# Twenty series of extra products in one group of layer 0's up projection

## The chip, the cores and the metric

The kernel runs on one core of one Trainium2 chip. The metric is the time of one execution in device microseconds (us). A core has a matrix engine, TensorE (PE in the profile), which multiplies a stationary operand of up to 128 columns (the weights, loaded ahead of each product; PEld in the profile) with the moving rows that stream past it and adds into PSUM; VectorE (DVE), ScalarE (ACT) and GpSimd (POOL) for elementwise work; and SyncE (SP), which here issues the loads of weights from HBM into SBUF, the on-chip memory. The engines run side by side and wait for each other by semaphores.

## The reference

A small decoder of two layers on 256 tokens, with 16 learned tokens put ahead of them, so that T = 272 rows; the width is 2048, with 16 heads of 128 and an MLP of 8192.

```python
for layer in range(DEPTH):
    a = rms_norm(h, norm_attn[layer])
    if layer < N_A_LAYERS:                      # layer 0
        proj = a @ fox_w_in[i]                  # q, k, v and forget gates
        o = forgetting_attention(...)
        h = h + o.reshape(b, length, D_MODEL) @ fox_w_o[i]
    else:                                       # layer 1
        c = rms_norm(h, kv_norm)
        k_s, v_s = jnp.split(c @ w_kv, 2, axis=-1)
        q = split_heads(a @ sb_w_q[i])
        o = stick_breaking_attention(q, shared_k, shared_v)
        h = h + o.reshape(b, length, D_MODEL) @ sb_w_o[i]
    h = h + squared_relu_mlp(rms_norm(h, norm_mlp[layer]), w_up[layer], w_down[layer])
return rms_norm(h, final_norm)[:, N_META:]
```

`squared_relu_mlp` is `jnp.square(jax.nn.relu(h @ w_up)) @ w_down`. Everything is float32.

## The kernel before

Activations are kept transposed, features on the 128 partitions and tokens along the row, in 16 chunks of 128 features. Every large matrix product goes through `gemm_group` (L173): one call makes 512 output features (four accumulators `acc`, one per 128 features, `m`) from all 2048 input features, in four steps `kb` of four chunks each. A float32 product is made of three products of a narrower type, float32r: both operands are split into a high part and the remainder, and high times high, high times low and low times high are added. So each pair of an input chunk `kc` and an accumulator `m` takes three products.

The activations lie split in a tile `x_...` made by `Split` (L99): per chunk 640 numbers of 4 bytes, in which the high part stands at `sp.hi` and the low part at `sp.lo`. 64 numbers are 256 bytes, and a chunk is ten such pieces. In layer 0, where the rows are 272 long (`t0` = 0), the high part begins at number 48 of a chunk and the low part at 368, so that both end at the end of a piece and touch five. In layer 1, where only the 256 rows of the tokens are needed (`t0` = 16), they begin at 0 and 320, at the beginning of a piece, and touch four.

The weights of a step `kb` come from HBM in two halves `raw` (512 KB each) on SP's queue (L197). ScalarE rounds a half into `whi` (L214) and VectorE writes the remainder into `wlo` (L215); each has two chunks of 512 columns. There are four buffers of `raw`, of `whi` and of `wlo`, that is two steps' worth. In layer 0 the weights begin at the beginning of a piece, so that the 128 columns of a product touch two pieces; in layer 1 they begin 16 numbers later and touch three.

The products are issued at L235 to L238 through `gemm_matmul` (L160). Once the first group is over, each product is tied behind the one before it (`queued`, `pinned`), so that TensorE's order in these groups is the order in which the code is written. The order of the steps: `kb` 0 and 3 run accumulator by accumulator over all four chunks, `kb` 1 and 2 run half by half (24 products on the first half's two chunks, then 24 on the second's), so that a buffer is given back as soon as a half is done. For `kb` = 3, `evac` follows each accumulator.

The MLP (`mlp`, L539) makes the 8192 hidden features in four parts `f`: for each part four groups of the up projection, whose `evac` multiplies by the norm's factor, squares and splits the result into `x_u`, and then four groups of the down projection, whose `evac` adds to the residual stream. The up projection of layer 0 reads `x_m`, which is complete before its second group starts.

Short-lived results in PSUM (scores, transposes, norms) share four buffers with the tag `patt`; the four accumulators have buffers of their own. At the start, nine products into an `idle` tile of that tag (L62) are read by nobody.

Of the kernel before, what the change touches and what calls it, by code (L numbers as in the profile page):

```python
# [2 lines left out]

# [6 lines left out]
F32 = mybir.dt.float32  # L10
# [5 lines left out]
P = 128  # L16
# [18 lines left out]
def yoco_kernel(ctx: ExitStack, tc: tile.TileContext, hT_in, gains, b_f, w_f, w_qkv0, w_o0, w_up, w_dn,  # L35
# [12 lines left out]
    patt = ctx.enter_context(tc.tile_pool(name="patt", bufs=4, space=bass.MemoryType.PSUM))  # L48
# [75 lines left out]
    class Norm:  # L124
# [15 lines left out]
        def finish(self):  # L140
# [13 lines left out]
            nc.vector.tensor_tensor(out=r[:, self.t0:], in0=y[:, :n], in1=t[:, :n], op=ALU.mult)  # L154
            return r

    uid = [0]
    queued, pinned = [], [False]

    def gemm_matmul(*args, **kw):  # L160

        ins = nc.tensor.matmul(*args, **kw).ins  # L162
        if queued and pinned[0]:
            tc.add_manual_dep(ins, queued[0].name, mybir.DependencyInfo(mybir.DependencyClass.NoSync,
                                                                        mybir.DependencyReason.DATA))
        queued[:] = [ins]
# [3 lines left out]
        tc.add_manual_dep(ins.ins, queued[0].name, mybir.DependencyInfo(mybir.DependencyClass.NoSync,  # L170
                                                                        mybir.DependencyReason.DATA))

    def gemm_group(wblk, sp, t0, evac, before={}, after={}, load_x=None, widen=False):  # L173

        uid[0] += 1
        u = uid[0]  # L180
        accs = [pacc.tile([P, 512], F32, tag="acc", name=f"acc_{u}_{m}") for m in range(4)]
        n = T - t0
        for kb in range(4):
            src_w = wblk[kb].rearrange("p (k c) -> p k c", k=4)
            if kb in before:
                before[kb]()
            piece = 1 if load_x is not None and kb < 2 else 2
            raws = [wraw.tile([P, 2, 512], F32, tag="raw", name=f"raw_{u}_{kb}_{hf}") for hf in range(2)]
            for k0 in range(0, 4, piece):
                if load_x is not None:  # L190
                    load_x(range(4 * kb + k0, 4 * kb + k0 + piece))
                if load_x is not None and kb == k0 == 0:

                    for c0 in (0, 256):
                        nc.scalar.dma_start(raws[0][:, 0, c0:c0 + 256], src_w[:, 0, c0:c0 + 256])
                else:
                    nc.sync.dma_start(raws[k0 // 2][:, k0 % 2:k0 % 2 + piece], src_w[:, k0:k0 + piece])  # L197
            parts = []
            for hf in range(2):
                whi = wspl.tile([P, 2 * 576], F32R, tag="whi", name=f"whi_{u}_{kb}_{hf}")  # L200
                wlo = wspl.tile([P, 2, 576], F32R, tag="wlo", name=f"wlo_{u}_{kb}_{hf}")
                if t0:
                    whi = whi.rearrange("p (k c) -> p k c", k=2)[:, :, 16:528]
                    wlo = wlo[:, :, 16:528]
                else:
                    whi = whi[:, :1024].rearrange("p (k c) -> p k c", k=2)
                    wlo = wlo[:, :, :512]
                boxes = [(o, piece, 0, 512) for o in range(0, 2, piece)]
                if load_x is not None and kb == hf == 0:
                    boxes[:1] = [(0, 1, 0, 256), (0, 1, 256, 512)]  # L210
                for o, no, c0, c1 in boxes:
                    src = raws[hf][:, o:o + no, c0:c1]
                    hp, lp = whi[:, o:o + no, c0:c1], wlo[:, o:o + no, c0:c1]
                    on_act = nc.scalar.activation(hp, src, AF.Copy)  # L214
                    on_dve = nc.vector.tensor_tensor(out=lp, in0=src, in1=hp.bitcast(F32), op=ALU.subtract)  # L215
                parts.append((whi, wlo))
            if kb in after:
                with tc.issue_after(on_act.ins), tc.issue_after(on_dve.ins):
                    after[kb]()


            if load_x is not None and kb == 0:
                runs = [([kc], range(4)) for kc in range(4)]
            elif kb in (0, 3):
                runs = [(range(4), [m]) for m in range(4)]
            else:
                runs = [(range(2 * hf, 2 * hf + 2), range(4)) for hf in range(2)]
            pinned[0] = load_x is None
            for kcs, ms in runs:
                if t0:  # L230
                    series = [(w, x, kc, m) for w, x in ((0, "hi"), (0, "lo"), (1, "hi")) for m in ms for kc in kcs]
                else:
                    series = [(w, x, kc, m) for m in ms for kc in kcs for w, x in ((0, "hi"), (0, "lo"), (1, "hi"))]
                for i, (w, x, kc, m) in enumerate(series):
                    over = SPAN if widen and kb == m == 0 and i in (0, 4, 8) else 0  # L235
                    rhs = sp.wide[x] if over else getattr(sp, x)[:, 4 * kb + kc]
                    gemm_matmul(accs[m][:, :n + over], parts[kc // 2][w][:, kc % 2, m * P:(m + 1) * P], rhs,
                                start=kb == kc == w == 0 and x == "hi", stop=kb == kc == 3 and w == 1)  # L238
                if kb == 3:
                    for m in ms:  # L240
                        evac(m, accs[m][:, :n])

    def residual_add(c, acc, t0):
        nc.vector.tensor_tensor(out=hT[:, c, t0:], in0=acc, in1=hT[:, c, t0:], op=ALU.add)  # L244
# [6 lines left out]
    def load_x(chunks):  # L251
        c0, n = chunks[0], len(chunks)
        nc.sync.dma_start(hT[:, c0:c0 + n, :], hT_in[:, c0:c0 + n, :])
        if c0 == 0:
            nc.sync.dma_start(g_sb, gains)
        for c in chunks:
            split_chunk(xa, G_A0, c)

    def first_norm(kb):
        if kb == 1:  # L260
            box["wf"] = load_gates()
        for c in range(4 * kb, 4 * kb + 4):
            norm.add(c)
# [171 lines left out]
    for g in range(4):  # L435
# [6 lines left out]
        if g == 0:  # L442

            gemm_group(w_qkv0[0], xa, 0, lambda m, acc, qT=qT: nc.scalar.copy(qT[:, m, :], acc),
                       after={kb: (lambda kb=kb: first_norm(kb)) for kb in range(4)}, load_x=load_x)
# [93 lines left out]
    def mlp(layer, xm, norm, t0, last_evac):  # L539
        box = {}  # L540

        def get_rstd():
            box["r"] = norm.finish()

        for f in range(N_FF):
            u = Split(f"u{layer}_{f}", t0)
            for g in range(4):
                def evac(m, acc, g=g):
                    c = 4 * g + m
                    r = tmp.tile([P, T], F32, tag="relu", name=f"relu_{layer}_{f}_{c}")  # L550
                    u2 = tmp.tile([P, T], F32, tag="u2", name=f"u2_{layer}_{f}_{c}")
                    nc.vector.scalar_tensor_tensor(out=r[:, t0:], in0=acc, scalar=0.0, in1=box["r"][:, t0:],
                                                   op0=ALU.max, op1=ALU.mult)
                    nc.scalar.activation(u2[:, t0:], r[:, t0:], AF.Square)
                    nc.scalar.activation(u.hi[:, c], u2[:, t0:], AF.Copy)
                    nc.vector.tensor_tensor(out=u.lo[:, c], in0=u2[:, t0:], in1=u.hi[:, c].bitcast(F32),
                                            op=ALU.subtract)
                gemm_group(w_up[layer, f, g], xm, t0, evac, {2: get_rstd} if f == g == 0 else {},
                           widen=t0 == M and g % 2 == 1)
            for g in range(4):  # L560
                def evac(m, acc, g=g):
                    residual_add(4 * g + m, acc, t0)
                    if f == N_FF - 1:
                        last_evac(4 * g + m)
                gemm_group(w_dn[layer, f, g], u, t0, evac, widen=t0 == M and g % 2 == 1)

    xm, norm_m = out_proj(w_o0, ao, 0, G_M0, "m0", late, turning)
# [4 lines left out]
    def after_layer0(c):  # L572
# [3 lines left out]
        norm1.add(c)  # L576

    mlp(0, xm, norm_m, 0, after_layer0)
    xq = box["xq"]
    xc = Split("kv", 0)  # L580
# [5 lines left out]
    for g in range(4):  # L586
# [4 lines left out]
        def split_c(kb, g=g):  # L591
            for c in ([4 * kb + g - 1] if g < 3 else [4 * kb + 2, 4 * kb + 3]):
# [3 lines left out]
                   after={kb: (lambda kb=kb: split_c(kb)) for kb in range(4)} if g else {}, widen=g > 0)  # L596
# [45 lines left out]
    xm, norm_m = out_proj(w_o1, ao, M, G_M1, "m1", late, turning)  # L642
# [12 lines left out]
    def last_evac(c):  # L655
        if c < NC - 4:
            normf.add(c)
        else:
            if c == NC - 4:
                add_squares(normf.acc, True, False)  # L660
            sq = tmp.tile([P, T], F32, tag="sq", name=f"sq_fin_{c}")
            nc.scalar.activation(sq[:, M:], hT[:, c, M:], AF.Square)
            add_squares(sq, False, c == NC - 1)
        if c < NC - 4:
            nc.scalar.activation(hT[:, c, M:], hT[:, c, M:], AF.Copy, scale=g_sb[:, G_FIN, c:c + 1])
# [3 lines left out]
    a, y, t, rs = (fin[:, i, :] for i in range(4))  # L669
# [81 lines left out]
```

## Time and profile before

| | us |
|---|---|
| median of two timed runs | 2279.29 (2278.92 to 2279.66) |
| the profiled execution, whole | 2278.99 |
| its span, first to last instruction | 2277.3 |
| TensorE busy with products | 2265.0 |
| VectorE busy | 1360.6 |
| ScalarE busy | 1111.8 |

The profile is of one execution. A row of a group of instructions gives the line, the engine, the operation, what it writes and reads with the numbers of the buffers left out, and then how many there were, their busy time together and the mean duration of one. A product's duration is not its price: products overlap, each begins while the one before it is still draining, and what one costs is the distance from its start to the next one's start. The time line gives start and length of runs of equal instructions in the order of time, in us from the start of the span.

### The profile page before, as it was taken

How to read it: one execution, taken by the hardware profiler on the slowest of the kernel's cores; microseconds unless marked ns; L12 is line 12 of the kernel's file. 1: busy time of each engine (PE TensorE's matmuls, PEld its weight loads, DVE VectorE, ACT ScalarE, POOL GpSimd, SP SyncE). 2: the span in 40 equal slices, each digit the busy share in tenths (PEclk: the TensorE clock that was granted, in tenths of full speed). 3: DMA queues.
4: the chain of work that ended last, by engine and by line, in shares of the span. 5: the costliest groups of instructions: out<-in, count | busy, mean ns of one | idle time of the engine just before them, and what ended most of it. 6: DMA issues, size and time to landing. Idle time of an engine off the chain costs nothing.

```text
span 2277.3 us, 44746 instructions
## 1 busy us (share of the span) xinstructions
PE 2265.0 (99%) x18882; PEld 2259.6 (99%) x18882; DVE 1360.6 (60%) x1909; ACT 1111.8 (49%) x1533; POOL 32.8 (1%) x75
## 2 busy tenths in 40 slices
PE   9999999999999999999999999999999999999998
PEld 9999999999999999999999999999999999999998
DVE  7777676555454455455566677766555555555554
ACT  6654554443354344344444567655544443544553
POOL 1000000000000000000000000000000000000000
PEclk9999999999999999999999999999999999999999
DMA  7555555555555555555565544455656656556563
GB/s 237 178 163 168 182 167 161 182 180 171 185 172 186 179 169 186 175 185 178 170 192 181 180 160 156 160 189 184 198 187 195 200 190 201 189 188 203 184 203 130
DMA packets 116905, 412.32 MB, mean 181 GB/s; under 512 B 13520, under 2 KB 16992, under 8 KB 116704
## 3 DMA queue, kind: packets, MB, share of 16 engines
q1 hardware_dynamic: 114560, 406.29, 55.3%
q10 hardware_dynamic: 2144, 3.17, 0.5%
q8 instruction: 148, 2.42, 0.4%
q14 instruction: 53, 0.43, 0.1%
HBM read 407.29 MB, written 2.11 MB: 180 GB/s over the span
## 4 chain that ended last, share of the span: by engine, by line
PE 99%; DMA 1%; DVE 0%; ACT 0%; issue 0%; DVEq 0%; SPq 0%; ACTq 0%
PE acc L162 96%; PE po L406 1%; PE ps L338 1%; DMA raw<-w_qkv 1%; PE ps L336 0%; PE po L409 0%; DMA hT<-hT_in 0%; PE po L410 0%; DVE ob L693 0%; PE pf L285 0%; PE pf L286 0%; ACT whi L214 0%; PE pms_fin L650 0%; DVE ob L690 0%; ACT x_o L430 0%; PE pms_a L143 0%
## 5 line engine op out<-in xcount | busy, mean ns | idle before, releaser
L215 DVE TENSOR_TENSOR wlo<-raw,whi 128x1024 fp32r<-128x1024 f32 (+1 forms) x773 | 927.4, 1216 | 674.1 <-ACT whi L214 666.9
L214 ACT ACTIVATE whi<-raw 128x1024 fp32r<-128x1024 f32 (+1 forms) x773 | 797.3, 1051 | 942.5 <-PE acc L162 909.5
L162 PE MATMUL acc<-x_m,whi 128*128 128x272 f32 (+1 forms) x4096 | 643.2, 281 | 0.0
L162 PE MATMUL acc<-x_u,whi 128*128 128x272 f32 (+1 forms) x4096 | 642.9, 281 | 0.0
L162 PEld LDWEIGHTS acc<-x_m,whi 128*128 128x128 f32 x4096 | 566.0, 188 | 0.1
L162 PEld LDWEIGHTS acc<-x_u,whi 128*128 128x128 f32 x4096 | 565.8, 188 | 0.0
L162 PE MATMUL acc<-x_m,wlo 128*128 128x272 f32 (+1 forms) x2048 | 440.9, 281 | 0.0
L162 PE MATMUL acc<-x_u,wlo 128*128 128x272 f32 (+1 forms) x2048 | 440.8, 281 | 0.0
L162 PE MATMUL acc<-x_a,whi 128*128 128x272 f32 (+1 forms) x2048 | 353.6, 286 | 0.5 <-ACT whi L214 0.4
L162 PEld LDWEIGHTS acc<-x_m,wlo 128*128 128x128 f32 x2048 | 323.4, 188 | 0.0
L162 PEld LDWEIGHTS acc<-x_u,wlo 128*128 128x128 f32 x2048 | 323.3, 188 | 0.0
L162 PEld LDWEIGHTS acc<-x_a,whi 128*128 128x128 f32 x2048 | 300.5, 188 | 1.5 <-ACT whi L214 1.3
L162 PE MATMUL acc<-x_a,wlo 128*128 128x272 f32 (+1 forms) x1024 | 253.1, 285 | 0.0
L162 PE MATMUL acc<-x_kv,whi 128*128 128x272 f32 x1024 | 192.6, 287 | 0.0
L162 PEld LDWEIGHTS acc<-x_a,wlo 128*128 128x128 f32 x1024 | 175.6, 188 | 0.7 <-issue 0.5
L162 PE MATMUL acc<-x_o,whi 128*128 128x272 f32 (+1 forms) x1024 | 162.6, 283 | 0.7 <-ACT x_o L430 0.4
L162 PEld LDWEIGHTS acc<-x_kv,whi 128*128 128x128 f32 x1024 | 160.0, 188 | 0.0
L162 PE MATMUL acc<-x_kv,wlo 128*128 128x272 f32 x512 | 147.1, 287 | 0.0
L162 PEld LDWEIGHTS acc<-x_o,whi 128*128 128x128 f32 x1024 | 142.0, 188 | 1.4 <-DVE x_o L431 0.7
L244 DVE TENSOR_TENSOR hT<-acc,hT 128x272 f32<-128x272 f32 (+1 forms) x160 | 69.1, 432 | 86.3 <-PE acc L162 86.2
L162 PE MATMUL acc<-x_o,wlo 128*128 128x272 f32 (+1 forms) x512 | 110.5, 282 | 0.0
L162 PEld LDWEIGHTS acc<-x_kv,wlo 128*128 128x128 f32 x512 | 96.5, 188 | 0.0
(180 smaller groups left out, 1062.0 us busy)
## 6 DMA issues: line engine op xcount, KB each, us to landing
raw<-w_up SPq DMA_DIRECT2D x256, 512.0 KB, 4.6
raw<-w_dn SPq DMA_DIRECT2D x256, 512.0 KB, 4.6
raw<-w_qkv SPq DMA_DIRECT2D x92, 512.0 KB, 3.8
raw<-w_o SPq DMA_DIRECT2D x64, 512.0 KB, 4.3
raw<-w_kv SPq DMA_DIRECT2D x64, 512.0 KB, 4.5
raw<-w_q SPq DMA_DIRECT2D x32, 512.0 KB, 4.7
fk<-f_dram ACTq DMA_DIRECT2D x4, 544.0 KB, 5.9
raw<-w_qkv SPq DMA_DIRECT2D x7, 256.0 KB, 4.9
```

Source lines behind the costliest of these rows:

```text
L162: ins = nc.tensor.matmul(*args, **kw).ins
L214: on_act = nc.scalar.activation(hp, src, AF.Copy)
L215: on_dve = nc.vector.tensor_tensor(out=lp, in0=src, in1=hp.bitcast(F32), op=ALU.subtract)
L244: nc.vector.tensor_tensor(out=hT[:, c, t0:], in0=acc, in1=hT[:, c, t0:], op=ALU.add)
L338: nc.tensor.matmul(ps[:, 144:416], qs[a][:, j, :], ks[b][:, j, :], start=i == 0, stop=i == 2)
L406: ins = nc.tensor.matmul(po[:, i, :], v[:, j, 0, :], p[:, j, :2 * P], start=i == 0, stop=False)
```

## The change

In one group of products, the second group (`g` = 1) of the first part (`f` = 0) of layer 0's up projection, at the beginning of step `kb` = 2, twenty series of 18 products each are put in, 360 in all. Each product of a series has the same two operands; a series sums up in one tile `push` with the tag `patt`, which nobody reads. Nothing else differs. The operands are the rows of `x_m`'s chunk 2 (`row`, 272 numbers from number 48 of the chunk), the first half's high weights `wa` used as rows, and as stationary weights either `near` (the first 128 columns of the low weights `wb`, adjacent), the same a few numbers further on, or `far`, 128 numbers of `x_m` that stand 64 numbers apart, so that each is in a piece of 256 bytes of its own. `lines(t, o, blk, n)` takes `n` runs of `blk` adjacent numbers, the runs 64 numbers apart.

| series | rows | stationary weights |
|---|---|---|
| 0 | 272 adjacent | near |
| 1 | 17 runs of 16 | near |
| 2, 3, 4, 5 | 272 adjacent | 128 adjacent, 4, 8, 56 and 60 numbers further on |
| 6 | 272 adjacent | every second of 256 |
| 7 | the first 256 of the same | near |
| 8, 9 | 256 adjacent, from the start of a piece | 16 numbers further on; far |
| 10, 11 | 16 runs of 16 | near; far |
| 12, 13 | 8 runs of 32 | near; far |
| 14, 15 | 512 adjacent | near; far |
| 16 | 16 runs of 32 | far |
| 17, 18 | 64 adjacent | near; far |
| 19 | 128 adjacent | near |

```diff
+    def probes(sp, parts, u):
+
+        (wa, wb), _ = parts
+        wa = wa.rearrange("p k c -> p (k c)")
+        lines = lambda t, o, blk, n: bass.AP(t.tensor, t.offset + o, [t.ap[0], [64, n], [1, blk]])
+        row = sp.hi[:, 2]
+        far = bass.AP(row.tensor, row.offset + 1, [row.ap[0], [64, P]])
+        near = wb[:, 0, 0:P]
+        kinds = [(row, near), (lines(row, 0, 16, 17), near),
+                 (row, wb[:, 0, 4:132]), (row, wb[:, 0, 8:136]), (row, wb[:, 0, 56:184]), (row, wb[:, 0, 60:188]),
+                 (row, bass.AP(near.tensor, near.offset, [near.ap[0], [2, P]])),
+                 (row[:, :256], near), (wa[:, :256], wb[:, 0, 16:144]), (wa[:, :256], far),
+                 (lines(wa, 0, 16, 16), near), (lines(wa, 0, 16, 16), far),
+                 (lines(wa, 0, 32, 8), near), (lines(wa, 0, 32, 8), far),
+                 (wa[:, :512], near), (wa[:, :512], far), (lines(wa, 0, 32, 16), far),
+                 (wa[:, :64], near), (wa[:, :64], far), (wa[:, :128], near)]
+        for i, (x, w) in enumerate(kinds):
+            t = patt.tile([P, 512], F32, tag="patt", name=f"push_{u}_{i}")
+            n = int(np.prod([k for _, k in x.ap[1:]]))
+            for k in range(18):
+                gemm_matmul(t[:, :n], w, x, start=k == 0, stop=k == 17)
...
             pinned[0] = load_x is None
+            if probe and kb == 2:
+                probes(sp, parts, u)
             for kcs, ms in runs:
...
-                gemm_group(w_up[layer, f, g], xm, t0, evac, {2: get_rstd} if f == g == 0 else {},
+                gemm_group(w_up[layer, f, g], xm, t0, evac, {2: get_rstd} if f == g == 0 else {}, probe=layer == 0 and f == 0 and g == 1,
                            widen=t0 == M and g % 2 == 1)
```

The programs of the two kernels differ in TensorE's order alone, and there in one place. Before, at the passage from step 1 to step 2 of this group (the group is number 18 of the program; `whi_18_1_1` is the high part of the second half of step 1, `whi_18_2_0` that of the first half of step 2; in brackets, the engine whose semaphore a product waits for):

```order
L162 MATMUL acc_18_3_5330<-x_m0_3919,whi_18_1_1_5399 128x272 x2
L162 MATMUL acc_18_3_5330<-x_m0_3919,wlo_18_1_1_5400 128x272
L162 MATMUL acc_18_0_5327<-x_m0_3919,whi_18_2_0_5455 128x272 [waits Activation_49]
L162 MATMUL acc_18_0_5327<-x_m0_3919,whi_18_2_0_5455 128x272
L162 MATMUL acc_18_0_5327<-x_m0_3919,wlo_18_2_0_5456 128x272 [waits DVE_49]
L162 MATMUL acc_18_0_5327<-x_m0_3919,whi_18_2_0_5455 128x272 x2
```

Step 2 waits first for the high part and, with its third product, for the low part. In the changed kernel, TensorE at the same place:

```order
L186 MATMUL acc_18_3_5330<-x_m0_3919,whi_18_1_1_5399 128x272 x2
L186 MATMUL acc_18_3_5330<-x_m0_3919,wlo_18_1_1_5400 128x272
L186 MATMUL push_18_0_5463<-x_m0_3919,wlo_18_2_0_5456 128x272 [waits DVE_49]
L186 MATMUL push_18_0_5463<-x_m0_3919,wlo_18_2_0_5456 128x272 x17
L186 MATMUL push_18_1_5482<-x_m0_3919,wlo_18_2_0_5456 128x272 [waits PE_49]
L186 MATMUL push_18_1_5482<-x_m0_3919,wlo_18_2_0_5456 128x272 x17
```

The series have moved in ahead of step 2, and the low part is now waited for first. From series 1 on, a series' first product waits for TensorE's own count (`PE_49`), by which the buffer of its `push` tile is known to be free; the high part is waited for by series 8. The end of the series, on TensorE, and the step that was there before:

```order
L186 MATMUL push_18_17_5786<-whi_18_2_0_5455,wlo_18_2_0_5456 128x64 [waits PE_49]
L186 MATMUL push_18_17_5786<-whi_18_2_0_5455,wlo_18_2_0_5456 128x64 x17
L186 MATMUL push_18_18_5805<-whi_18_2_0_5455,x_m0_3919 128x64 [waits PE_49]
L186 MATMUL push_18_18_5805<-whi_18_2_0_5455,x_m0_3919 128x64 x17
L186 MATMUL push_18_19_5824<-whi_18_2_0_5455,wlo_18_2_0_5456 128x128 [waits PE_49]
L186 MATMUL push_18_19_5824<-whi_18_2_0_5455,wlo_18_2_0_5456 128x128 x17
L186 MATMUL acc_18_0_5327<-x_m0_3919,whi_18_2_0_5455 128x272 x2
L186 MATMUL acc_18_0_5327<-x_m0_3919,wlo_18_2_0_5456 128x272
```

Step 2 now begins without a wait, since both its parts were waited for by the series. The orders of the other engines and of the queues are the same in both.

More of the change, by code (lines that the diff above doesn't have):

```diff
@@ L1 @@
 import math
+import numpy as np
 from contextlib import ExitStack
@@ L171, in behind, with gemm_group @@
                                                                         mybir.DependencyReason.DATA))
-    def gemm_group(wblk, sp, t0, evac, before={}, after={}, load_x=None, widen=False):
+    def gemm_group(wblk, sp, t0, evac, before={}, after={}, load_x=None, widen=False, probe=False):
         uid[0] += 1
```

## The prediction

> **What bounds the kernel now.** I read the page's busy times first, then the chain that ended last, then the place of the change in the time line.
>
> ```profile
> span 2277.3 us, 44746 instructions
> PE 2265.0 (99%) x18882; PEld 2259.6 (99%) x18882; DVE 1360.6 (60%) x1909; ACT 1111.8 (49%) x1533; POOL 32.8 (1%) x75
> PEclk9999999999999999999999999999999999999999
> PE 99%; DMA 1%; DVE 0%; ACT 0%; issue 0%; DVEq 0%; SPq 0%; ACTq 0%
> L162 PE MATMUL acc<-x_m,whi 128*128 128x272 f32 x2048 | 379.3, 287 | 0.0
> ```
>
> TensorE is busy for 99% of the span at its full clock, the chain is TensorE for 99%, and the products of the up projection (the last row, from the groups kept apart by shape) have no idle time ahead of them. VectorE and ScalarE are busy for 60% and 49%. So whatever is added to TensorE's order is paid in full, unless something elsewhere makes it wait less, and there is hardly a wait to save. The chain inside the stretch of the change, and TensorE's time line there:
>
> ```profile
> 430.84 39.22 PE acc L162 x318
> 454.24 0.28 PE L162 MATMUL acc<-x_m,wlo 128*128 128x272 f32 x1
> 454.24 0.31 PEld L162 LDWEIGHTS acc<-x_m,whi 128*128 128x128 f32 x2
> 454.36 0.41 PE L162 MATMUL acc<-x_m,whi 128*128 128x272 f32 x2
> ...
> 456.46 0.28 PE L162 MATMUL acc<-x_m,wlo 128*128 128x272 f32 x1
> ```
>
> The first row is a piece of the chain: 318 products in 39.22 us without any wait, 123.3 ns each. A product lasts 287 ns but the next one starts 123.3 ns later, and that distance is its price. The other rows show it again: one product in three has `wlo` as weights, from 454.24 to 456.46 there are 18 products (six rounds of three), 2.22 us or 123.3 ns each. The product at 454.36 is the first of step `kb` = 2 of group 18: the series go in ahead of it.
>
> **What the rest of the kernel does meanwhile.** The first added product needs the low weights of this step's first half, which VectorE writes.
>
> ```profile
> 448.87 2.36 DVE L215 TENSOR_TENSOR wlo<-raw,whi 128x1024 fp32r<-128x1024 f32 x2 [2.68 <-ACT whi L214]
> 452.57 1.23 DVE L215 TENSOR_TENSOR wlo<-raw,whi 128x1024 fp32r<-128x1024 f32 x1 [1.34 <-ACT whi L214]
> ```
>
> The two instructions at 448.87 write both halves of step 2 (their buffers come free when step 0 ends) and are over at 451.23, 3.1 us ahead of 454.36. So the new order of the waits, low part first, costs nothing. Series 4 to 19 wait for TensorE's own count from the series four earlier, since four buffers carry the tag: 54 products lie between, about 6 us, and the wait is over before it is met. While the series run, ScalarE, VectorE and SP fill their buffers and stop; they were waiting for TensorE there anyway. Nothing is queued behind a wait of another engine. That they start the next step with full buffers is worth nothing either, with 0.0 idle on TensorE to save.
>
> **What a series costs.** The same products are in the trace for 272 adjacent rows. For 256 rows, from layer 1's up projection:
>
> ```profile
> 1807.70 1.07 PE L162 MATMUL acc<-x_m,whi 128*128 128x256 f32 x8
> 1808.60 0.62 PE L162 MATMUL acc<-x_m,wlo 128*128 128x256 f32 x4
> ...
> 1811.78 0.39 PE L162 MATMUL acc<-x_m,whi 128*128 128x256 f32 x2
> ```
>
> From 1807.70 to 1811.78 there are 36 products (three rounds of 8 and 4): 113.3 ns each. Their rows begin at a piece and fill four; the 272 begin at number 48 and touch five. The step from 256 to 272 costs 10.0 ns for 16 columns. At the average of the 256, 113.3 / 256 = 0.443 ns, 16 columns are 7.1 ns, so 2.9 ns are left for the one piece more. That is my price for opening a piece in the moving rows; its ends are nothing, and 10.0 ns for every run of 16 as if each were that fifth piece.
>
> The weights have their own limit, the load ahead of each product:
>
> ```profile
> L162 PEld LDWEIGHTS acc<-x_m,whi 128*128 128x128 f32 x4096 | 566.0, 188 | 0.1
> L285 PEld LDWEIGHTS pf<-x_a,wf 128*32 128x32 f32 x16 | 1.7, 108 | 0.2
> L285 PE MATMUL pf<-x_a,wf 128*32 128x272 f32 x16 | 4.1, 287 | 0.0
> ```
>
> 128 columns take 188 ns, 32 take 108: 80 ns for 96 columns, 0.83 ns a column, and so 107 ns for the 128 behind a fixed part that overlaps. This is below 113.3 and 123.3, so the load is hidden today. Of layer 0 and layer 1 (windows around the two stretches above):
>
> ```profile
> L162 PEld LDWEIGHTS acc<-x_m,whi x21: 187/189/189, 452.8 to 456.5; 128*128 128x128 f32 x21
> L162 PEld LDWEIGHTS acc<-x_m,whi x56: 187/188/188, 1802.1 to 1811.1; 128*128 128x128 f32 x56
> ```
>
> In layer 0 the 128 weights lie in two pieces, in layer 1 in three, and the load is the same to 1 ns. A piece more costs a load at most about that.
>
> Now the sum, in us per series of 18.
>
> - Series 0 and 2 to 5: 2.22 each, 11.10. Series 0 is today's product; the others move the weights by a few numbers, two pieces become three, hidden as in layer 1.
> - Series 6, every second weight: four pieces, 2.22, since no row shows that four differ from three. Its upper end is a load of twice 107 ns, 214 ns, 3.85.
> - Series 1: 17 pieces instead of 5, 123.3 + 12 x 2.9 = 158.1 ns, 2.85 (ends 123.3 and 17 x 10.0 = 170 ns: 2.22 to 3.06).
> - Series 7: 256 rows from number 48, five pieces, midway between 113.3 and 123.3: 2.13. Series 8: as in layer 1, 2.04.
> - Series 10: 16 pieces, 113.3 + 12 x 2.9 = 148.1 ns, 2.67 (2.04 to 2.88). Series 12: 8 pieces, 113.3 + 4 x 2.9 = 124.9 ns, 2.25 (2.04 to 2.40, midway to 16 pieces).
> - Series 14: 512 rows, twice 113.3 = 226.6 ns, 4.08.
> - Series 17 and 19: 64 and 128 rows are shorter than a load, so the load sets the pace, 107 ns: 1.93 each, 3.85 (no float32r product so narrow is in the trace; the lower end is the rival on narrow products below, the upper end the rate of a plain float32 product, 0.83 ns a column, which changes only series 19, and that by nothing, as 128 columns again take 107).
>
> These fourteen series: 33.2 us.
>
> The six with far weights (9, 11, 13, 15, 16, 18) open a piece with every column: 128 pieces where the trace has three. The lower end is a load that does not notice, 107 ns. The upper end is the 2.9 ns of the moving rows for each column, 371 ns. I take 0.83 ns, one column's time, on top of each column's 0.83, so 214 ns: it is the row of the loads that is nearest, and its third piece costs at most about 1 ns. Then series 9, 11, 13 and 18 are paced by the load at 214 ns, 3.85 each, 15.4; series 15 by its 512 rows, 226.6 ns, 4.08; series 16 by 512 rows in 16 pieces, 226.6 + 8 x 2.9 = 249.8 ns, 4.50. Together 24.0 us.
>
> 33.2 + 24.0 = 57.2 us on top of the profiled execution of 2278.99 (0.3 below the median of the two timed runs, which is inside their spread): **2336 us**, 2.5% longer. About 2% (45.6 us) is what a measurement of this kernel can tell from no change.
>
> [...]
>
> **The rivals.**
>
> *The layout of weights is free.* The load takes 107 ns wherever its columns lie. For it: 188 ns with two pieces and with three. Against it: three pieces are far from 128. Then series 9, 11, 13, 15, 16 and 18 cost what their rows or the plain load cost, 2.04 + 2.67 + 2.25 + 4.08 + 4.50 + 1.93 = 17.5, and the sum is 50.7 us: 2330. If runs of rows are free as well, series 1, 10, 11, 12, 13 and 16 fall by 0.63, 0.63, 0.63, 0.21, 0.21 and 0.42, 2.7 together: 2327. Against that speaks the fifth piece's 2.9 ns. [...]
>
> *Each far column pays what a piece costs the rows.* The load is 371 ns, beyond any of the six's rows, and they cost 6.68 us each, 40.1 in all. 33.2 + 40.1 = 73.3 us: 2352. For it: the rows do pay for a piece. Against it: the loads pay at most about 1 ns for theirs, and rows of 272 with 32 weight columns in one piece last 287 ns like those with 128 in two, so the two streams are not seen to disturb each other. If a column cost as much as a run of 16 rows, 10.0 ns, a load would take 1.28 us and the change 171 us; nothing in the trace speaks for that.
>
> *Narrow products keep their weights, and the whole stays within 2%.* The 18 products of a series have the same weights. If TensorE did not load them again in series 17, 18 and 19, their rows would set the pace, 64 x 0.443 = 28 ns and 57 ns for 128: 0.51, 0.51 and 1.02 instead of 1.93 each, 3.75 us less. On top of the layout being free altogether, 47.9 - 3.8 = 44.2 us: 2323, not slower by 2%. It decides once these 54 products cost less than 64 ns on average (2.3 us less). Against it:
>
> ```profile
> L62 PEld LDWEIGHTS idle<-mean_w x18: 288/333/333, 1.1 to 4.7; 128*128 128x128 f32 x18
> L62 PE MATMUL idle<-mean_w x18: 421/421/582, 1.1 to 4.9; 128*128 128x128 f32 x18
> ```
>
> Nine products with the same weights (two passes each) have 18 loads, one for each pass.
>
> *The series are dropped,* as nobody reads `push`: 2279. The same two rows speak against it, since nobody reads `idle` either and its products run.
>
> **How the numbers follow.** The forecast has 0.38. The layout of weights being free has 0.31, the price of the rows for each far column 0.19, dearer columns still (2360 and more) 0.05, narrow products that keep their weights 0.06, dropped series 0.01. From 2326, just below the cheapest of the layout being free, to 2356, some us above the dear far columns, the range holds the first three. Faster by over 2% is left 0.01; within 2% are the last two, less a little for narrow products that keep their weights under a dearer layout: 0.06; slower by over 2%: 0.93.
>
> **What would show it.** The span grows by what lies between the first `push` product and the first of step 2. TensorE should show no idle time there or behind it, and 19242 products, 360 more. Series 0 and 2 to 5 should have starts 123 ns apart, series 8 113, series 14 227, and series 17 and 19 about 107. Series 18 is the far load laid bare: 107 there means that the layout is free, 214 the forecast, 371 the price of the rows. Series 9 against 15 shows the same under 256 and 512 rows, series 10 and 12 against 8 the price of a piece in the rows. What would make the forecast wrong is above all that load, which carries 6.5 us to the lower case and 16.1 to the upper; then float32r products of 64 or 128 rows being slower per column than 0.83 ns, which no row excludes.

## The result and the profile after

The changed kernel takes **2338.15 us** (2337.83 to 2338.48, two runs) against 2279.29 before: 58.9 us more, a ratio of 1.0258 (95% interval 1.0214 to 1.0302). The forecast was 2336, 57 us more, in a range of 2326 to 2356. The profiled execution took 2338.48 us. From the page of the changed kernel: the span, busy times, the granted clock, and the chain by engine.

```profile
span 2336.8 us, 45467 instructions
PE 2324.8 (99%) x19242; PEld 2318.7 (99%) x19242; DVE 1359.8 (58%) x1909; ACT 1111.4 (48%) x1533; POOL 32.7 (1%) x75
PEclk9999999999999999999999999999999999999999
PE 99%; DMA 1%; DVE 0%; ACT 0%; issue 0%; DVEq 0%; SPq 0%; ACTq 0%
```

360 products more, TensorE 59.8 us busier, the span 59.5 us longer, the other engines as before. The chain in a window around the place (start, length, what), and TensorE's time line there (start, length, line, operation, tiles, how many):

```profile
439.92 14.67 PE acc L186 x119
454.60 58.47 PE push L186 x360
513.07 6.95 PE acc L186 x49
```

```profile
454.44 18.10 PE L186 MATMUL push<-x_m,wlo 128*128 128x272 f32 x144
472.37 2.22 PE L186 MATMUL push<-whi,wlo 128*128 128x256 f32 x18
474.43 4.19 PE L186 MATMUL push<-whi,x_m 128*128 128x256 f32 x18
...
494.69 8.60 PE L186 MATMUL push<-whi,x_m 128*128 128x512 f32 x36
503.13 2.09 PE L186 MATMUL push<-whi,wlo 128*128 128x64 f32 x18
505.05 4.11 PE L186 MATMUL push<-whi,x_m 128*128 128x64 f32 x18
508.98 4.08 PE L186 MATMUL push<-whi,wlo 128*128 128x128 f32 x18
512.86 0.76 PE L186 MATMUL acc<-x_m,whi 128*128 128x272 f32 x2
```

No product waits: no row has an idle time in brackets, and the series take 512.86 - 454.44 = 58.4 us in one piece. So the change costs what its products cost one after another, as forecast. Per series, from the products' starts (a series' first to the next series' first, by 18):

| series | rows, weights | forecast ns | measured ns |
|---|---|---|---|
| 0 | 272 adjacent, near | 123 | 123.3 |
| 1 | 17 runs of 16, near | 158 | 126.4 |
| 2, 3, 4, 5 | 272, shifted weights | 123 | 126.6, 123.4, 125.4, 126.6 |
| 6 | 272, every second weight | 123 | 126.6 |
| 7 | 256 from number 48, near | 118 | 118.1 |
| 8 | 256 from 0, weights from 16 | 113 | 114.3 |
| 10, 12 | 16 runs of 16, 8 of 32, near | 148, 125 | 122.7, 117.7 |
| 14 | 512, near | 227 | 228.8 |
| 17 | 64, near | 107 | 107.0 |
| **19** | **128, near** | **107** | **215.7** |
| 9, 11, 13 | 256 in three layouts, far | 214 | 223.6, 216.0, 216.8 |
| 18 | 64, far | 214 | 218.2 |
| 15, 16 | 512, 16 runs of 32, far | 227, 250 | 233.3, 235.5 |

The far load is close to the forecast's value everywhere. Two things are not: the price of a piece in the rows, and series 19. Series 17 meets its 107.0 ns by its first start alone: the first two starts are 30 ns apart, the others 109 to 112. TensorE in three windows (width, busy, products, granted clock, then DMA):

```profile
500.00:507.97 7.97, 7.97 (x46) 1.00 0.01 2
507.97:514.79 6.82, 6.82 (x33) 0.50 0.00 0
514.79:520.00 5.21, 5.21 (x44) 1.00 0.00 0
```

The granted clock falls to half inside series 18 and comes back 6.82 us later, inside step 2. The page's row of the clock does not show it, since one of its slices is 58 us long. Series 19 lies inside, and so do step 2's first products: from 512.86 nine of them take 2.06 us (to 514.92), where nine at 123.3 ns take 1.11.

To compare kernels below, I take the stretch from the first product behind step 1 to the 120th of the group's own products behind that, the series included, by the products' starts: 14.80 us before, 74.18 after, 59.4 more.

### The profile page after: what moved, and what is told of

Same layout as the page of the kernel before. It is cut to its first block, busy times and chain, and to the rows that moved or that the text cites. A ratio compares the mean times of both kernels' runs of the same rounds, so it can differ in the third digit from the quotient of the medians.

```text
span 2336.8 us, 45467 instructions
## 1 busy us (share of the span) xinstructions
PE 2324.8 (99%) x19242; PEld 2318.7 (99%) x19242; DVE 1359.8 (58%) x1909; ACT 1111.4 (48%) x1533; POOL 32.7 (1%) x75
## 4 chain that ended last, share of the span: by engine, by line
PE 99%; DMA 1%; DVE 0%; ACT 0%; issue 0%; DVEq 0%; SPq 0%; ACTq 0%
PE acc L186 94%; PE push L186 3%; PE po L432 1%; PE ps L364 1%; DMA raw<-w_qkv 1%; PE ps L362 0%; PE po L435 0%; DMA hT<-hT_in 0%; PE po L436 0%; DVE ob L719 0%; PE pf L312 0%; PE pf L311 0%; ACT whi L238 0%; PE pms_fin L676 0%; DVE ob L716 0%; ACT x_o L456 0%
```

## Experiments

Two questions stayed open: why 128 rows took twice 107 ns, and what in the layout of 256-byte pieces costs time, since weights that step from piece to piece cost twice a load (216 to 224 ns) while rows in runs cost almost nothing (3.1 ns for 12 pieces more in series 1). The experiments change `probes` alone. Near weights for far, the run without the narrow series and the mixed order were run four times each, the others once; all prices per product are from one profiled execution, and most of them from one series of 18.

### Series 19 ahead of the 64-row series

```diff
+        kinds = kinds[:17] + kinds[19:] + kinds[17:19]
```

> The series of 128 rows (19) moved ahead of the two series of 64 rows (17, 18); all else as in the changed kernel. Clock theory: in the changed kernel series 19 took 213 ns a product because the granted clock had fallen to 0.50 behind the 64-row series. Ahead of them it runs at full clock, 107 to 112 ns a product, 2.0 us instead of 3.9; if the clock falls at all, it falls in series 18 or in step 2's own products. Width theory: a float32r product of 128 rows takes 1.67 ns a row whatever the clock; series 19 stays at 213 ns with a granted clock of 1.00.

Series 19 now starts at 502.34, series 17 at 504.30, series 18 at 506.27. TensorE in windows:

```profile
502.34:504.30 1.96, 1.96 (x20) 1.00 0.00 0
504.30:507.65 3.35, 3.35 (x27) 1.00 0.00 0
507.65:514.48 6.83, 6.83 (x32) 0.50 0.00 0
```

128 rows take 1.96 us, 109 ns a product, at full clock. The width theory falls. The clock falls all the same, now across series 18 and the real products behind it, which take 227 ns each until it is back. 2336.77 us in one run; the stretch is 73.39 us, 0.8 less than in the changed kernel: the half clock has moved from added products onto the kernel's own.

### Near weights instead of far

```diff
+        kinds = [(x, near if w is far else w) for x, w in kinds]
```

> The six series with far weights get the near ones. Theory of the load (a far load takes about 214 ns and sets the pace): series 9, 11, 13 and 18 fall from 224, 216, 217 and 218 ns to 113, 123, 118 and 107 to 112 ns, series 15 and 16 hardly change (512 rows hide the load); 7.4 us less, about 2331 us. If the clock no longer falls, 2.8 us less again, about 2328. Theory of the rows (far weights slow the rows that stream): series 15 and 16 gain about as much per product as series 9, 100 ns, 3.6 us more.

2330.68 us (2329.89 to 2332.76), ratio 1.0231 (1.0214 to 1.0248): the 2331 of the load theory with the clock still falling, and it does fall:

```profile
496.62:501.63 5.01, 5.01 (x47) 1.00 0.00 0
501.63:508.46 6.83, 6.83 (x33) 0.50 0.00 0
508.46:512.00 3.54, 3.54 (x31) 1.00 0.00 0
```

Series 9, 11, 13 and 18 go from 224, 216, 217 and 218 ns to 120, 122, 118 and 112. Series 15 goes from 233 to 227 and series 16 from 236 to 237: under 512 rows the far load was hidden but for some 7 ns. So far weights cost a longer load, and do not slow the rows that stream meanwhile by more than that. Two misses in the expectation: series 9 with near weights takes 120 ns, not 113, of which more below; and the gain over the changed kernel is 74.18 - 67.29 = 6.9 us in the stretch, not 7.4. Most of the missing 0.5 us is the half clock: step 2 now runs under it for longer and loses 2.35 us to it instead of 0.95, series 19 loses 0.95 instead of 1.92.

### Without the narrow series

```diff
+        kinds = kinds[:17]
```

> Series 17, 18 and 19 are left out. Clock theory: the granted clock stays at 1.00 through the series and into step 2, whose first eight products cost 123 instead of 227 ns; 1.93 + 3.93 + 3.88 us of the series and about 0.95 us behind them go, about 2327.5 us. Width theory: only the series' own 9.7 us go, about 2328.4, and step 2's first products stay slow for some other reason.

2326.82 us (2326.33 to 2327.57), ratio 1.0212 (1.0197 to 1.0227), 48.2 us over the kernel before. TensorE through the series, and behind them:

```profile
453.89:502.58 48.69, 48.69 (x308) 1.00 0.08 26
502.58:505.00 2.42, 2.42 (x21) 1.00 0.00 0
```

The clock stays at 1.00, the first real product behind the series takes 125 ns, and the stretch is 63.50 us, 10.68 less than in the changed kernel: 9.74 of the three series and 0.94 behind them. By the timing alone, 10.7 and 9.7 could hardly be told apart; the trace tells them.

### The step between weights

```diff
...
+        first = sp.hi[:, 0]
+        every = lambda t, o, k: bass.AP(t.tensor, t.offset + o, [t.ap[0], [k, P]])
+        adj = wb[:, 0, :256]
+        kinds = [(adj, every(wa, 16, 1))] + [(adj, every(wa, 0, k)) for k in (1, 2, 3, 4, 5, 6, 8)]
+        kinds += [(adj, every(row, 0, 64)), (adj, far), (adj, every(first, 0, 80))]
```

> Eleven series of 18, all with the same 256 adjacent rows, differ in the weights' step alone: 1 (from number 16 and from 0), 2, 3, 4, 5, 6, 8, 64 (from an even and from an odd start), 80. Line theory (what lies in one line of 16 bytes is loaded together, two to a line at full pace): 113 ns for steps 1 and 2, about 160 for 3 (96 lines), 214 to 224 for 4, 5, 6, 8, 64 and 80 alike. Piece theory (0.87 ns for each piece of 256 bytes opened): 113 to 121 ns up to step 8 (at most 16 pieces), 214 to 224 only for 64 and 80 (128 pieces).

By the starts, steps 1 (from 16), 1 (from 0), 2, 3, 4, 5, 6, 8, 64, 64 (odd start) and 80 take 114, 120, 120, 173, 233, 229, 229, 242, 223, 223 and 222 ns a product. The loads themselves, from windows inside the series of steps 1 (from 16), 2, 3, 4 and 64 (number; duration in ns as lowest, median, highest; first and last start):

```profile
L183 PEld LDWEIGHTS push<-wlo,whi x18: 187/188/189, 453.9 to 455.8; 128*128 128x128 f32 x18
L183 PEld LDWEIGHTS push<-wlo,whi x17: 195/195/197, 458.2 to 460.1; 128*128 128x128 f32 x17
L183 PEld LDWEIGHTS push<-wlo,whi x17: 261/262/262, 460.4 to 463.2; 128*128 128x128 f32 x17
L183 PEld LDWEIGHTS push<-wlo,whi x18: 317/330/333, 463.3 to 467.3; 128*128 128x128 f32 x18
L183 PEld LDWEIGHTS push<-wlo,x_m x18: 317/317/318, 484.1 to 487.9; 128*128 128x128 f32 x18
```

From step 4 on, each number lies in a line of 16 bytes (four numbers) of its own, and the price is there in full: 233 ns with 8 pieces of 256 bytes, 223 with 128 pieces, 222 to 242 over all these steps. The piece theory falls. By lines: step 3 touches 96 lines in 173 ns, step 4 128 in 233, step 64 128 in 223, about 1.8 ns a line each time; step 2 touches 64 lines, which at 1.8 ns is 115 ns, and takes 120, no more than step 1 from 0. The line is a way of counting, which no trace shows as such; the times from step 3 on fit it. With two weights to a line the load takes 195 ns against 188 from number 16, with one the product takes about twice as long (222 to 242 ns against 114 to 120). A load that goes by its number of columns alone, as in the rival of the free layout, is what these steps show only up to step 2.

### The layout of the rows

```diff
...
+        run = lambda t, o, *d: bass.AP(t.tensor, t.offset + o, [t.ap[0], *[list(k) for k in d]])
+        w = wb[:, 0, 16:144]
+        kinds = [(wa[:, o:o + 256], w) for o in (0, 8, 16, 32, 48, 56)]
+        kinds += [(wa[:, o:o + 272], w) for o in (0, 16, 32, 48)]
+        kinds += [(run(wa, 0, (2, 256)), w), (run(wa, 0, (4, 128), (1, 2)), w), (run(wa, 0, (4, 256)), w),
+                  (run(row, 0, (64, 32), (1, 8)), w), (run(row, 0, (64, 64), (1, 4)), w),
+                  (run(row, 0, (64, 128), (1, 2)), w), (run(row, 0, (64, 128), (8, 2)), w)]
```

> Seventeen series of 18 with the same adjacent weights, differing in the rows. 256 adjacent rows from number 0, 8, 16, 32, 48, 56 of a piece; 272 from 0, 16, 32, 48; then 256 rows as every second number, as pairs 4 apart, as every fourth number, as 32 runs of 8, 64 runs of 4, 128 runs of 2 (each run in a piece of its own), and as 128 times two numbers 8 apart. Start theory (the fifth piece costs by where the rows begin or end, not by its being a piece): 113 ns from 0, 117 to 119 from every other start, 272 at 120 to 128; a piece with two or more numbers to a 16-byte line costs little, 113 to 125 ns for all the runs. Piece theory with the price that the changed kernel showed (0.3 to 1.0 ns a piece): 32 runs 122 to 141, 64 runs 131 to 173, 128 runs 150 to 237. One number to a line (every fourth; two numbers 8 apart) is about twice as slow, 214 or more, by the line theory, and 113 to 120 (every fourth) without it. The forecast's 2.9 ns a piece would make 194, 287 and 473 of the runs.

256 adjacent rows: 114 ns from number 0 and 118 to 119 from 8, 16, 32, 48 and 56, as the start theory has it. 272 rows: 123 from 0, 125 from 16, 127 from 32 and 48. Every second number 228, pairs 4 apart 229, every fourth 233; 32 runs of 8 142, 64 runs of 4 146, 128 pairs in 128 pieces 287. Windows of 256 rows from 0, of 272 from 0, of every second number, of 32 runs of 8, of the 128 pairs, and of the end of the last series:

```profile
453.31:455.36 2.05, 2.05 (x20) 1.00 0.87 284
466.00:468.22 2.22, 2.22 (x20) 1.00 0.00 0
475.04:479.15 4.11, 4.11 (x21) 1.00 0.00 0
487.48:490.03 2.55, 2.55 (x20) 1.00 0.00 0
492.65:497.82 5.17, 5.17 (x21) 0.94 0.00 0
500.58:501.76 1.18, 1.18 (x7) 1.00 0.00 0
```

Both theories miss the pairs, and the start theory the runs as well (142 and 146 ns against at most 125). Rows with two numbers to a line of 16 bytes are twice as slow as adjacent ones (228 and 229 against 114 ns), where weights with two to a line are not (120 ns a product, as with adjacent ones from 0), so two to a line, enough for the weights, are not enough for the rows. Every fourth number, one to a line and so twice the lines, costs no more (233 ns), so the rows have no price by the line as the weights have. With four to a line (runs of 4) the price is 146 ns in 64 pieces. The last series, two numbers 8 apart, took 219 ns. Most of it lay under a half clock (0.50 from 497.17 to 500.58), but its last five products, from 500.67 on, are at full clock and still 218 to 220 ns apart: one number to a line in 128 pieces is cheaper here than adjacent pairs in as many pieces, and no theory of this run says why. The clock had fallen in the series of the pairs, whose 256 rows, at the 114 ns of adjacent ones, fill 40% of their 287 ns.

### Runs in few and in many pieces

```diff
...
+        kinds = [(run(wa, 0, (32, 16), (1, 16)), w), (run(wa, 0, (64, 16), (1, 16)), w),
+                 (run(wa, 0, (16, 32), (1, 8)), w), (run(wa, 0, (32, 32), (1, 8)), w), (run(row, 0, (64, 32), (1, 8)), w),
+                 (run(wa, 0, (8, 64), (1, 4)), w), (run(wa, 0, (16, 64), (1, 4)), w), (run(row, 0, (64, 64), (1, 4)), w),
+                 (run(wa, 0, (4, 128), (1, 2)), w), (run(wa, 0, (8, 128), (1, 2)), w), (row, near), (row, near),
+                 (run(row, 0, (64, 128), (1, 2)), w), (row, near), (row, near), (row, near)]
+        kinds += [(wa[:, :256], wb[:, 0, o:o + 128]) for o in (0, 8, 16, 32, 48, 64)]
```

> 256 rows in runs, with the same weights, each length of run laid out in a different number of pieces of 256 bytes: 16 runs of 16 in 8 and 16 pieces, 32 runs of 8 in 8, 16 and 32, 64 runs of 4 in 8, 16 and 64, 128 runs of 2 in 8, 16 and 128. Piece theory: the time grows with the pieces at one length of run. Run theory (the length of the run alone decides, a gap costs the same wherever it leads): 16 runs of 16 at 123 ns, 32 runs of 8 at 142, 64 runs of 4 at 145, 128 runs of 2 at 229 in any number of pieces; only the 128 runs in 128 pieces were seen at 287. The last six series have 256 adjacent rows and weights from number 0, 8, 16, 32, 48 and 64 of their piece: 120 ns from 0 and 114 from 16 are known; no theory, a measurement of how much the weights' start moves.

| 256 rows as | ns a product (pieces) |
|---|---|
| 16 runs of 16 | 120.0 (8), 120.2 (16) |
| 32 runs of 8 | 118.2 (8), 119.3 (16), 127.8 (32) |
| 64 runs of 4 | 117.2 (8), 121.0 (16), 145.8 (64) |
| 128 runs of 2 | 228.7 (8), 233.2 (16), 287.3 (128) |

Windows of the runs of 4 in 8, 16 and 64 pieces:

```profile
464.61:466.72 2.11, 2.11 (x20) 1.00 0.00 0
466.72:468.90 2.18, 2.18 (x21) 1.00 0.00 0
468.90:471.52 2.62, 2.62 (x20) 1.00 0.00 0
```

Neither theory holds whole. A gap costs nothing as long as whole lines are read and the pieces are few: runs of 4, 8 and 16 in 8 pieces are all at 117 to 120 ns, as adjacent rows from some starts are. The layouts in many pieces do cost more, by about 0.5 ns a piece: (145.8 - 121.0) / 48 = 0.5 from 16 to 64, (287.3 - 233.2) / 112 = 0.5 from 16 to 128. That it is the pieces is not shown, for three reasons: the layouts in 32 pieces and more are read from `x_m`, from number 48, instead of from `whi`; the same 32 runs of 8 took 141.8 ns in the run on the layout of the rows and 127.8 here, so one such number is worth some 10%; and the two numbers 8 apart of that run, in 128 pieces too, took 219 ns, less than any layout here with two numbers to a line.

The last six series, 256 adjacent rows from 0 with weights from 0, 8, 16, 32, 48 and 64: 119.4, 117.9, 113.6, 118.4, 117.7 and 119.6 ns. Only 16 reaches 114, the start that layer 1's weights have. Why is open.

### Blocks of narrow products

```diff
...
+        for n, w, k in ((224, near, 72), (192, near, 72), (160, near, 72), (128, near, 72), (96, near, 72),
+                        (64, near, 72), (256, far, 40), (128, far, 40), (512, far, 40)):
+            kinds += [(row, near, 72), (wa[:, :n], w, k)]
+        kinds += [(row, near, 72)]
...
```

> Nine blocks, each of one kind of product, with 72 products of 272 rows ahead of each and behind the last (8.9 us, to bring the clock back): 72 products of 224, 192, 160, 128, 96 and 64 rows with near weights (8 us each at 107 to 112 ns), and 40 of 256, 128 and 512 rows with far weights. Clock theory: the granted clock falls to 0.50 in the blocks whose rows keep the array busy for a small part of the time: 64 near (27 of 112 ns, 24%) and 128 far (53 of 218 ns, 24%) for certain, 512 far (91%), 224 and 192 near (83%, 71%) not; the limit lies between. Where the clock is 1.00, all near blocks go at 107 to 113 ns a product. Width theory: 128 rows at 213 ns and 160 to 224 rows at 1.67 ns a row at a clock of 1.00.

The nine blocks in order, from a block's first product to the next block's:

```profile
462.38:470.42 8.04, 8.04 (x75) 1.00 0.00 0
479.31:487.32 8.01, 8.01 (x74) 1.00 0.00 0
496.23:504.23 8.00, 8.00 (x74) 1.00 0.01 2
513.39:521.38 7.99, 7.99 (x75) 1.00 0.01 2
530.31:542.17 11.86, 11.86 (x74) 0.66 0.01 1
553.64:564.97 11.33, 11.33 (x74) 0.69 0.01 1
575.39:584.31 8.92, 8.92 (x42) 1.00 0.01 2
593.21:601.95 8.74, 8.74 (x43) 0.82 0.01 2
612.61:622.04 9.43, 9.43 (x43) 1.00 0.01 2
```

224, 192, 160 and 128 rows all take 111 to 112 ns a product: the load's pace, whatever the rows. The clock holds down to 128 rows (1.00) and falls with 96 and 64 (0.66 and 0.69 over their blocks), and with 128 rows under a far load (0.82), though 128 rows under a near one keep it. So it is not the width of the product but how much of the time its rows fill: 128 rows, at the 0.447 ns a row worked out below, are 51% of 112 ns and 26% of 218. TensorE is busy without a gap in all nine blocks.

### Where the limit lies, and how long it takes

```diff
...
+        for n, k in ((120, 72), (112, 72), (104, 72), (96, 72), (64, 24), (64, 36), (64, 48)):
+            kinds += [(row, near, 108), (wa[:, :n], near, k)]
+        kinds += [(row, near, 72)]
...
```

> Blocks of 72 products of 120, 112, 104 and 96 rows (8 us each), then of 24, 36 and 48 products of 64 rows (2.7, 4.0 and 5.4 us), all with near weights and with 108 products of 272 rows (13.3 us) ahead of each and 72 behind the last. Share theory (the clock falls where the rows fill less than some share of the time; by the blocks before, 48% keeps it for 128 rows and 37% does not for 96, rows counted at 0.42 ns): the clock falls in the blocks of 96 and perhaps 104 rows (39%), not in that of 120 (45%). Time theory (it takes a stretch of that kind of 3.4 us, measured in fixed windows): 24 products of 64 rows never lower it, 48 may and 36 may or may not, since a whole window has to fall into them. Count theory (the number of short products decides): the block of 24 lowers it as well.

Windows of the blocks of 104 and of 96 rows, and of the half clock that begins in the latter; of 24 products of 64 rows and the products behind them; of the half clock behind the 36; and of the 48 and the half clock behind them:

```profile
509.86:517.84 7.98, 7.98 (x75) 1.00 0.00 0
531.23:543.07 11.84, 11.84 (x75) 0.66 0.01 1
534.95:548.60 13.65, 13.65 (x64) 0.50 0.00 1
...
558.99:561.59 2.60, 2.60 (x27) 1.00 0.00 0
561.59:575.00 13.41, 13.41 (x111) 1.00 0.00 1
...
579.32:582.74 3.42, 3.42 (x17) 0.50 0.00 0
593.91:599.18 5.27, 5.27 (x50) 1.00 0.00 0
599.80:603.22 3.42, 3.42 (x18) 0.50 0.00 0
```

One row takes (228.8 - 114.3) / 256 = 0.447 ns of streaming, from series 14 and 8. By that, 104 rows fill 42% of their 110.8 ns and keep the clock, as do 112 and 120; 96 rows fill 38% of 112 ns and lose it, and the 128 pairs above, 256 rows in 287 ns, at 40%, lost it as well. The limit lies at 40 to 42%, if a row is counted so; with series 9's 119.9 ns under near weights, the weights of series 14, a row takes (228.8 - 119.9) / 256 = 0.425 ns and the limit lies at 38 to 40%.

24 products of 64 rows (2.6 us) did not lower the clock; 36 (3.9 us) and 48 (5.3 us) lowered it for 3.42 us each, which begin 0.4 and 0.6 us after the last of them, in products that fill the time. The count theory falls: 24 short products keep the clock, and the 18 of the pairs lost it. The time theory holds in one half: the clock of this run changes at 534.95, 548.60, 579.32, 582.74, 599.80 and 603.22, whole multiples of 3.413 us apart, as it would with the time cut into windows of that length. But a whole window need not fall into the short products. Counted back by that length, and by the starts, the window up to 579.32 holds 27 of the 36 and 3 products of 272 rows, (27 x 64 + 3 x 272) x 0.447 ns = 1.14 us or 33% of it; the one up to 599.80 holds 25 of the 48 and 5 of 272, 39%; and the one that has all of the 24 (558.84 to 562.26) holds 6 of 272 beside them, 41%. One product of 272 more or less at an end is worth 4%. So by this count it matters how much of such a window the rows fill, and where the windows lie among the products is chance: the 128 pairs lost the clock where a whole window (493.76 to 497.17) lay among them and kept it in the run on pieces (1.00 from 484.30 to 489.48). The 6.82 us at 0.50 in the changed kernel are two such windows (2 x 3.413 = 6.83).

### The same products in another order

```diff
-        for i, (x, w) in enumerate(kinds):
+        for group in [(i,) for i in range(14)] + [(14, 17), (15, 18), (16,), (19,)]:
+            ts = {i: patt.tile([P, 512], F32, tag="patt", name=f"push_{u}_{i}") for i in group}
...
+                for i in group:
...
```

> The same 360 products in another order: series 14 and 17 take turns product by product, then 15 and 18, then come 16 and 19. Clock theory: no stretch of 3.4 us is short of rows any more, the granted clock stays at 1.00, series 19 takes 2.0 us instead of 3.9 and step 2's first products 123 ns instead of 227: 2.9 us less, about 2335.3 us. If the products themselves were slow whatever the clock, the time stays at 2338.

The series, series 19 apart, and the products behind:

```profile
454.75:509.59 54.84, 54.84 (x344) 1.00 0.06 23
509.59:511.55 1.96, 1.96 (x19) 1.00 0.00 0
511.55:514.00 2.45, 2.45 (x22) 1.00 0.00 0
```

The clock stays at 1.00 throughout, series 19 takes 1.96 us, and the stretch is 71.66 us, 2.5 less than in the changed kernel; 0.2 of what is missing to 2.9 is series 16, which takes 4.43 us instead of 4.24. The timing is 2336.36 us (2335.62 to 2337.19), ratio 1.0253 (1.0235 to 1.0271), 57.8 us over the kernel before against 58.9: the direction expected, but 1 to 2 us are at the edge of what the timing resolves. It is the trace that shows the mechanism.

## Why the prediction was right

**TensorE pays for everything.** Right: no idle time in the series or behind them, and the 58.4 us of the series reach the end whole.

**Waits.** Right: the low part was ready, and the waits for TensorE's own count cost nothing that the starts show; series 4 and 5, the first to wait so, take 125.4 and 126.6 ns a product, and series 2, which waits for a count long past, 126.6.

**Today's shapes.** Series 0, 7, 8 and 14 came within 2.2 ns of the forecast. Shifted weights were put at nothing and cost up to 3.3 ns a product, 0.2 us over five series; why is open.

**A piece in the rows, 2.9 ns.** Wrong by a factor of about ten: 12 pieces more cost 126.4 - 123.3 = 3.1 ns in series 1, 0.26 each. The step from 256 to 272 rows was read as 16 columns and one piece. Series 10 and 12, at 122.7 and 117.7 ns, are hardly above 120 ns or below it, which is what 256 adjacent rows take with the same weights (the near-weights run); the 113 ns that I counted from belongs to weights that start at 16. The term was 0.6, 0.5, 0.1 and 0.3 us too dear in series 1, 10, 12 and 16, 1.4 us in all.

**The far load, 214 ns.** Right in size, 216 to 224, but by luck of the choice: I had chosen the value for an opening of one column's time for each piece, and weights at step 4, in 8 pieces, cost no less (233 ns) than in 128 (223). What steps 3 and 4 fit instead is about 1.8 ns for each line of 16 bytes (173 ns for 96 lines, 233 for 128). That the rows are hardly slowed, on which the rival of the dear columns was marked down, is shown by series 15: 512 rows took 233.3 ns under far weights and 228.8 under near ones (series 14).

**Narrow products, 107 ns.** A little low: 64 to 224 rows go at 108 to 112 ns under near weights, and series 17's 107.0 is luck, by its first start. Series 19 was at 215.7 the one large error, 2.0 us; 128 rows do cost 109 to 111 ns, but at half the clock a near load takes twice as long, 213 ns from start to start. (A far load does not: series 18 takes 218 ns on either side of the change of clock at 507.97.) The clock was taken as given at 1.00; that the added products could change it is the step that was missing, and none of the rivals had it. It cost 1.9 us in series 19 and 0.95 us behind the series. The 0.83 ns a column that the forecast gave for a plain float32 product is about what the trace of the kernel before shows in the `po<-pt,vt` of 256 rows (two in the 0.42 us from 110.94 to 111.36, 0.82 ns a row). The forecast did name slower narrow products as a risk, but by their width, which the run with series 19 moved ahead rules out. A sign may have stood in the prediction's own lines: the loads of `idle` at the start take 333 ns, like those of series 19 under the half clock, against 188 elsewhere, though the trace of the kernel before has no granted clock below 1.00 there.

**The sum.** 57.2 us forecast, 58.4 measured in the series and 59.4 with what followed. That the total is so close is in part luck: the rows' price being 1.4 us too high hid half of the clock's 2.9. The rivals: a free layout of weights fell with series 18 (218 ns), the dear columns with the same, weights kept with series 17 (107 ns a product for 29 ns of rows), dropped series with 19242 products.

## What to carry to other kernels

A product's price was, in these runs, about the longer of its load and its rows (107 to 112 ns for 64 to 224 rows under a near load, 216 to 224 for 256 under a far one; where the two were close, up to 10 ns more: 256 rows took 114 to 120 ns under a load of 111), and it can be read from the distance of starts; where only one side changes, look at whether the other hides it. Stationary weights were cheap here with two or more to a line of 16 bytes (120 ns a product at step 2, 222 to 242 with one to a line), moving rows only with four to a line (117 ns in runs of four in 8 pieces, 229 in pairs in as many). Where in memory those lines are mattered little for the weights (233 ns in 8 pieces, 223 in 128) and for rows in 8 and 16 pieces (117.2 and 121.0 ns in runs of four); runs of four in 64 pieces and pairs in 128 took some 20% longer than in 16 (145.8 against 121.0 ns, 287.3 against 233.2). And a busy engine need not have its full clock: behind windows of 3.4 us of which the rows filled 33% and 39% it was 0.50 for 3.42 us, behind one of 41% it stayed at 1.00, so it is worth trying short products between long ones, which here kept it at 1.00 and took 2.5 us less for the same 360.

## What the runs showed of the hardware that was not expected

- The clock halved under an engine that was busy without a gap: 64 rows in 112 ns (26% streaming) or 128 rows under a far load (26%) lowered it to 0.50, 104 rows in 111 ns (42%) did not. Its changes lie whole multiples of 3.413 us apart and go with how much of the window just over was filled (33% and 39% lost it, 41% did not), so the products that pay may be others.
- Weights and rows differ in what a line of 16 bytes costs: weights with two of its four numbers used load at almost full pace (195 against 188 ns), rows so read take twice as long (228 against 114 ns), and with one of four no longer than that (233 and 219 ns).
- 256 adjacent rows take 113.6 ns with weights from number 16 of a piece and 117.7 to 119.6 with weights from 0, 8, 32, 48 or 64. The load alone does not ask for it: with weights from 0, 224 rows and fewer go at 111 to 112 ns. The cause is open.
